# Transposing the second layer's q and k with VectorE and GpSimd in place of TensorE, in a two-layer encoder trunk

## The chip, the core and the metric

The kernel runs on one core of one Trainium2 chip. The engines are named as in the profile: PE is TensorE (PEld its weight load), DVE VectorE, ACT ScalarE, POOL GpSimd, SP the engine whose queue issues the loads. The metric is the device time in microseconds of one execution, and lower is better. Kernels are compared by the median of several runs.

## The reference, cut to what matters

Two layers, 256 tokens, 2048 channels, all in float32. Each layer normalises and modulates its input, multiplies it by one wide matrix, and gets from that two attention mixers and two gates; after the gated merge comes an output projection and a gated feed-forward part with a short convolution. The change is in the second layer's q and k, between their norm and the scores:

```python
h = rmsnorm(x, norm_mix[l]) * (1.0 + sc_a) + sh_a
qa, ka, va, qb, kb, vb, ga, gb = split_cols(h @ w_in[l])
qa = rotary_partial(rmsnorm(qa.reshape(B, S, HA, HEAD_DIM), qn_a[l]), pos)
ka = rotary_partial(rmsnorm(ka.reshape(B, S, GA, HEAD_DIM), kn_a[l]), pos)
ya = window_attention(qa, ka, va, sink_a[l]) @ w_proj_a[l]
qb = rmsnorm(qb.reshape(B, S, HB, HEAD_DIM), qn_b[l])
kb = rmsnorm(kb.reshape(B, S, HB, HEAD_DIM), kn_b[l])
yb = neighbourhood_attention(qb, kb, vb, rel_bias_b[l]) @ w_proj_b[l]
merged = jax.nn.sigmoid(ga) * ya + jax.nn.sigmoid(gb) * yb
```

Mixer A has 8 query heads and 2 key heads of 128 channels, mixer B 8 and 8.

## The kernel before

**The stream of weights.** All matrices are read once, as 128x128 blocks in the order in which they are used. Sixteen blocks are a unit. `unit_steps` loads a unit (SP's queue), and splits each of its halves into two tiles: a cast by ACT (L319, `hl<-w`) and the difference between the weights and that cast by DVE (L320). A product is then three matmuls, high by high, high by low and low by high. The half units are called by layer, unit and half: `hl1_35_0` is the first half of unit 35 of the second layer. There are four such buffers, so the cast of a half can begin when PE has left the half two units earlier.

**q, k and v.** In the second layer units 0 to 7 belong to gate columns; units 8 to 43 make nine groups of 512 columns, four units each (`Stream.tokens`, L399 to L401, 24 matmuls a unit, into PSUM tiles `ps1_8` to `ps1_40`): group 0 holds both k heads of A and v, groups 1 and 2 the q heads of A; 3 and 6 are k of B, 5 and 8 q of B, 4 and 7 v of B. Then the gate units follow.

**Work in the background.** After each unit `Stream.tick` runs what was deferred by one tick and moves background jobs on by their rates (`Paced`). For a group of q or k, `qk_rows` sums squares per head on ACT (L569), takes roots (`qss` on DVE, L462, and `qrs` on POOL, L463), and three ticks later multiplies by the roots on DVE (`norm`, L578, into `qn`), with the rotary part for mixer A. One tick later `turn` transposes head by head on PE into PSUM (`qtp`, L602), and ACT writes the result with the gain to its place (L603). `qn` has one buffer.

**The heads.** `attention` starts a head when its groups are ready and moves all live heads on by one step at a time, `ATT` steps a tick. A head splits q and k into high and low parts (`in_halves`, `split`: ACT L411, DVE L412), makes scores on PE (`sc`, L629), a softmax on DVE and ACT (L632 to L648), transposes the probabilities, and multiplies by v (`po`, L667). In the second layer the probabilities are already transposed off PE, for all heads: `turned_blocks` transposes 32x32 blocks on DVE (L293) and moves the blocks with 16 copies on POOL (L298, `p<-packA`, `p<-packB`, `p<-spare`), and one step later `split` makes `pT` of them. The transposed rows of a head lie where q of the two heads before was, so DVE's transposition waits until POOL has copied the head before.

**The order.** Each engine runs its instructions in the order of the built program. The framework puts them in an order of its own from the priorities and dependences; `tc.keep_in_program_order` holds single instructions where the program has them.

Of the kernel before, what the change touches and what calls it, by code (L numbers as in the profile page):

```python
# [9 lines left out]
F32 = mybir.dt.float32  # L10
# [5 lines left out]
P = 128  # L16
# [4 lines left out]
HEAD = 128  # L21
# [57 lines left out]

H_RATE = [2.7, 1.7]  # L80

ATT = [1.288, 0.43]
ATT_B = [0.21, 0.4]

SCORES_3 = (1,)

MOVED = [(0,0), (8,8)]
STEPS = [1, 1]

# [49 lines left out]
def encoder(ctx: ExitStack, tc: tile.TileContext, a: dict, out: bass.AP):  # L139
# [144 lines left out]
    def later(n, fn):  # L284
# [3 lines left out]
        else:  # L288
            bg.defer(lambda: later(n - 1, fn))

    def turned_blocks(src, rows, n):

        nc.vector.transpose(out=rows, in_=src)  # L293
        blocks = rows.rearrange("p t (n k) -> p n t k", n=n)
        dst = src.rearrange("p t (n k) -> p (t n k)", n=n).rearrange("p (n t k) -> p n t k", n=n, t=2)
        for b in range(0, P, BLOCK):
            for a in range(0, P, BLOCK):
                nc.gpsimd.tensor_copy(  # L298
                    out=dst[a : a + BLOCK, :, :, b : b + BLOCK], in_=blocks[b : b + BLOCK, :, :, a : a + BLOCK]
                )  # L300

    def unit_steps(l, u, by_halves=False):

# [101 lines left out]
                    self.tick()  # L405
            return pss

    def split(dst, src, scale=None):

        if scale is None:  # L410
            nc.scalar.copy(dst[:, 0], src)  # L411
            nc.vector.tensor_tensor(out=dst[:, 1], in0=src, in1=dst[:, 0].bitcast(F32), op=ALU.subtract)  # L412
            return
        nc.scalar.activation(out=dst[:, 0], in_=src, func=AF.Copy, scale=scale)
        nc.vector.scalar_tensor_tensor(
            out=dst[:, 1], in0=src, scalar=scale, in1=dst[:, 0].bitcast(F32), op0=ALU.mult, op1=ALU.subtract
        )
# [140 lines left out]
            nc.vector.tensor_tensor(out=z[:], in0=ps[:, :S], in1=self.rbs[:], op=ALU.mult)  # L558
            return z, sh

    def qk_rows(pss, heads, rot, gain, dst, then):

        cols = 0
        n = heads * HEAD
        ss = sm.tile([P, 8], F32, name="qss", tag="qss")
        for t, ps in enumerate(pss):
            for i in range(heads):
                sq = at.tile([P, HEAD], F32, name="qsq", tag="qsq", bufs=1)
                nc.scalar.activation(  # L569
                    out=sq[:], in_=ps[:, cols + i * HEAD : cols + (i + 1) * HEAD], func=AF.Square,  # L570
                    accum_out=ss[:, t * heads + i : t * heads + i + 1],
                )
        rs = sm.tile([P, 8], F32, name="qrs", tag="qrs")
        rsqrt(rs[:, : 2 * heads], ss[:, : 2 * heads], HEAD, 2 * heads)
        def norm():
            qn = at.tile([P, 2, 4, HEAD], F32, name="qn", tag="qn", bufs=1)
            for t, ps in enumerate(pss):
                nc.vector.tensor_tensor(  # L578
                    out=qn[:, t, :heads],
                    in0=ps[:, cols : cols + n].rearrange("p (h d) -> p h d", d=HEAD),  # L580
                    in1=rs[:, t * heads : (t + 1) * heads].unsqueeze(2).broadcast_to([P, heads, HEAD]),
                    op=ALU.mult,
                )
            if rot is not None:
                x1, x2 = qn[:, :, :heads, :HALF], qn[:, :, :heads, HALF:ROT]
# [12 lines left out]
        def turn(qn):  # L598
            for t in range(2):
                ps = ax.tile([P, 4, P], F32, name="qtp", tag="ax")  # L600
                for h in range(heads):
                    nc.tensor.transpose(ps[:, h], qn[:, t, h], ident[:])  # L602
                nc.scalar.activation(  # L603
                    out=dst[:, :, t * P : (t + 1) * P], in_=ps[:, :heads], func=AF.Identity, scale=gain
                )
            then()

        bg.defer(lambda: bg.defer(lambda: bg.defer(norm)))
# [15 lines left out]
    def attend(q, k, v, p, mask, scale, sink, o, rows=None):  # L624

        sc = ax.tile([P, 2, S], F32, name="sc", tag="ax")
        for t in range(2):
            for i, j in by(q):
                nc.tensor.matmul(sc[:, t], q[i][:, t * P : (t + 1) * P], k[j], start=i + j == 0, stop=(i, j) == by(q)[-1])  # L629
        m = sm.tile([P, 2], F32, name="m", tag="m")  # L630
        for t in range(2):
            nc.vector.tensor_tensor_reduce(  # L632
                out=p[:, t], in0=sc[:, t], in1=mask[:, t], scale=scale, scalar=-3.0e38 if sink is None else sink,
                op0=ALU.add, op1=ALU.max, accum_out=m[:, t : t + 1],
            )
        nm = sm.tile([P, 2], F32, name="nm", tag="nm")
        nc.vector.tensor_scalar(out=nm[:], in0=m[:], scalar1=-1.0, scalar2=None, op0=ALU.mult)
        den = sm.tile([P, 2], F32, name="den", tag="den")
        for t in range(2):
            nc.scalar.activation(out=p[:, t], in_=p[:, t], func=AF.Exp, bias=nm[:, t : t + 1], accum_out=den[:, t : t + 1])  # L640
        if sink is not None:
            es = sm.tile([P, 2], F32, name="es", tag="es")
            nc.scalar.activation(out=es[:], in_=nm[:], func=AF.Exp, bias=sink)
            nc.vector.tensor_tensor(out=den[:], in0=den[:], in1=es[:], op=ALU.add)
        ri = sm.tile([P, 2], F32, name="ri", tag="ri")
        nc.vector.reciprocal(out=ri[:], in_=den[:])
        for t in range(2):
            nc.scalar.activation(out=p[:, t], in_=p[:, t], func=AF.Copy, scale=ri[:, t : t + 1])  # L648
# [12 lines left out]
        split(pT, tp[:])  # L661
        v = v()
        yield
        po = ax.tile([P, 512], F32, name="po", tag="ax")
        for i, j in by(v):
            for b in range(2):
                nc.tensor.matmul(po[:, :S], v[i][:, b], pT[:, j, b], start=i + j + b == 0, stop=i + b == 2)  # L667
# [118 lines left out]
    for l in range(L):  # L786
# [87 lines left out]

        def attention():

            todo = [(3, head_a, i) for i in range(HA)] + [(6 + 3 * (i // 4), head_b, i) for i in range(HB)]
            live = []
            while todo or live:
                for head in list(live):  # L880
                    if next(head, bg) is bg:
                        live.remove(head)
                        heads[0] += 1
                if todo and ready[0] >= todo[0][0]:
                    live.append(todo[0][1](todo[0][2]))
                    next(live[-1])
                    todo.pop(0)
                yield
# [15 lines left out]
        for pi, (groups, gates) in enumerate(parts):  # L904
            last = pi == len(parts) - 1
            for g, part in enumerate(groups):
# [21 lines left out]
                    for t in range(2):  # L928
                        nc.scalar.copy(rows[:, t, vcol:], pss[t][:, vcol:])
                if g == 0:  # L930
                    qk_rows(pss, GA, rots[1], gains[:, 1:2], kTa, turned)
                elif g < 3:
                    qk_rows(pss, 4, rots[0], gains[:, 0:1], dst, turned)
                elif vcol is None:
                    qk_rows(pss, 4, None, gains[:, 3:4] if g in (3, 6) else gains[:, 2:3], dst, turned)
                else:
                    turned()
                if g == 2:
                    bg.add(job, ATT[l])


# [240 lines left out]
```

## Time and profile before

| | us |
|---|---|
| median of 3 runs | 2658.42 (2656.88 to 2659.82) |
| the profiled execution's own time | 2660.64 |
| its span in the profile | 2658.7 |

The page gives the busy time of each engine, groups of instructions by line, and the chain of work that ended last. A timeline row has the start in us from the span's beginning, the duration, engine, line, operation, output and inputs, a count, and in brackets the idle time before it with what ended it. A waits row names who waited for whom, the total, the number of times and the longest. A windows row has the window and its length, then busy time and count for PE, PEld, DVE, ACT and POOL, the granted clock, DMA's share and GB/s.

### The profile page before, as it was taken

To read this page: it belongs to the slowest core of one execution; us is meant where nothing else is said; L and a number is where in the kernel's file an instruction comes from. 1 tells how busy PE (TensorE), PEld (TensorE's weight loads), DVE (VectorE), ACT (ScalarE), POOL (GpSimd) and SP (SyncE) were. 2 spreads that over 40 slices of the span, in tenths; PEclk is the share of its full clock that TensorE was granted. 3 is DMA by queue.
4 is the path that set the end of the run, shared out by engine and by line. 5 is a ranking of instruction groups with operands and counts; after the bars stand their busy time and mean duration, and the time that the engine had idled before them with its cause. 6 is when DMAs were issued, how large, how long until landed. Compare 5 with 4: busy or idle time off the path is not lost.

```text
span 2658.7 us, 51010 instructions
## 1 busy us (share of the span) xinstructions
PE 2646.4 (100%) x21192; PEld 2561.3 (96%) x21192; DVE 2116.5 (80%) x2975; ACT 1407.9 (53%) x2284; POOL 194.0 (7%) x281
## 2 busy tenths in 40 slices
PE   9999999999999999999999999999999999999999
PEld 7888899999999999999998889999999999999999
DVE  8898998897987888788886677868888866655664
ACT  5445865456653555355554566645565445544553
POOL 0001100000000000000000177610000000000000
PEclk9999999999999999999999999999999999999999
DMA  9988779885778788877856666766747775555554
GB/s 359 350 329 300 257 296 353 319 327 193 283 294 297 282 293 296 297 288 285 296 213 255 237 236 235 255 256 260 279 180 286 295 254 191 191 197 193 196 190 143
DMA packets 102042, 700.43 MB, mean 263 GB/s; under 512 B 12721, under 2 KB 15025, under 8 KB 17969
## 3 DMA queue, kind: packets, MB, share of 16 engines
q1 hardware_dynamic: 101810, 697.17, 71.3%
q8 instruction: 166, 2.72, 0.4%
q14 instruction: 66, 0.54, 0.1%
HBM read 695.03 MB, written 2.10 MB: 262 GB/s over the span
## 4 chain that ended last, share of the span: by engine, by line
PE 88%; DVE 5%; POOL 2%; ACT 2%; DMA 1%; issue 1%; DVEq 0%; ACTq 0%; POOLq 0%
PE ps L336 26%; PE ps L338 26%; PE ps L337 26%; PE ps_t L401 3%; PE ps_t L400 3%; PE ps_t L399 3%; POOL p L298 2%; DVE hl L320 2%; DMA aw<-in_aw 1%; DVE aw L230 1%; ACT hl L319 1%; PE sc L629 1%; PE po L667 1%; POOL qrs L463 0%; ACT qsq L569 0%
## 5 line engine op out<-in xcount | busy, mean ns | idle before, releaser
L320 DVE TENSOR_TENSOR hl<-w,hl 128x1024 fp32r<-128x1024 f32 x928 | 1129.8, 1224 | 308.6 <-ACT hl L319 304.6
L319 ACT CAST hl<-w 128x1024 fp32r<-128x1024 f32 x928 | 969.7, 1048 | 704.7 <-PE ps L338 494.0
L336 PE MATMUL ps<-h,hl 128*128 128x256 f32 x3328 | 922.5, 277 | 1.3 <-DVE ya L948 0.6
L337 PE MATMUL ps<-h,hl 128*128 128x256 f32 x3328 | 919.7, 276 | 0.0
L338 PE MATMUL ps<-h,hl 128*128 128x256 f32 x3328 | 919.6, 277 | 0.0
L336 PEld LDWEIGHTS ps<-h,hl 128*128 128x128 f32 x3328 | 624.8, 188 | 2.3 <-DVE ya L948 0.8
L337 PEld LDWEIGHTS ps<-h,hl 128*128 128x128 f32 x3328 | 625.2, 188 | 0.4 <-DVE h L492 0.2
L338 PEld LDWEIGHTS ps<-h,hl 128*128 128x128 f32 x3328 | 624.3, 188 | 0.0
L230 DVE CUSTOM_DVE_ANT_0 aw<-aw,cact,ab 128x2048 f32<-128x2048 f32 x189 | 443.8, 2349 | 73.8 <-DMA aw<-in_aw 73.4
L399 PE MATMUL ps_t<-hl,h 128*128 128x512 f32 x576 | 223.4, 393 | 2.1 <-ACT h L491 1.6
L400 PE MATMUL ps_t<-hl,h 128*128 128x512 f32 x576 | 224.9, 391 | 0.4
L401 PE MATMUL ps_t<-hl,h 128*128 128x512 f32 x576 | 224.3, 390 | 0.0
L1027 DVE SCALAR_TENSOR_TENSOR u<-ps,cw,u 128x255 f32<-128x255 f32 x304 | 146.1, 481 | 63.0 <-ACT u L1025 58.9
L1025 ACT ACTIVATE u<-ps,cw 128x256 f32<-128x256 f32 x152 | 85.7, 564 | 157.0 <-PE ps L338 156.9
L336 PE MATMUL ps<-merged,hl 128*128 128x256 f32 x512 | 141.8, 278 | 0.8 <-DVE m L425 0.8
L338 PE MATMUL ps<-merged,hl 128*128 128x256 f32 x512 | 141.7, 277 | 0.0
L337 PE MATMUL ps<-merged,hl 128*128 128x256 f32 x512 | 141.7, 277 | 0.0
L337 PE MATMUL ps<-act_o,hl 128*128 128x256 f32 x512 | 141.4, 276 | 0.0
L338 PE MATMUL ps<-act_o,hl 128*128 128x256 f32 x512 | 141.4, 276 | 0.0
L336 PE MATMUL ps<-act_o,hl 128*128 128x256 f32 x512 | 141.2, 276 | 0.0
L399 PEld LDWEIGHTS ps_t<-hl,h 128*128 128x128 f32 x576 | 107.9, 188 | 25.4 <-ACT h L491 2.6
L400 PEld LDWEIGHTS ps_t<-hl,h 128*128 128x128 f32 x576 | 108.1, 188 | 24.0 <-DVE hl L320 2.1
(239 smaller groups left out, 4774.5 us busy)
## 6 DMA issues: line engine op xcount, KB each, us to landing
w<-in_ws SPq DMA_DIRECT2D x463, 1024.0 KB, 4.9
aw<-in_aw SPq DMA_DIRECT2D x189, 1024.0 KB, 6.1
p<-in_bias SPq DMA_DIRECT2D x16, 256.0 KB, 4.5
x<-in_xT SPq DMA_DIRECT2D x4, 512.0 KB, 5.4
aw_o<-in_aw SPq DMA_DIRECT2D x2, 1024.0 KB, 12.5
out<-x SPq DMA_DIRECT2D x16, 128.0 KB, 2.2
w<-in_ws SPq DMA_DIRECT2D x2, 512.0 KB, 11.8
aw_b<-in_aw SPq DMA_DIRECT2D x1, 1024.0 KB, 17.1
```

Of the source, the lines that this page charges most:

```text
L230: nc.vector.tensor_tensor_reduce(out=raw[:], in0=raw[:], in1=cact[:], scale=1.0, scalar=ab[:, i : i + 1], op0=ALU.mult, op1=ALU.add, accum ...
L298: nc.gpsimd.tensor_copy(out=dst[a : a + BLOCK, :, :, b : b + BLOCK], in_=blocks[b : b + BLOCK, :, :, a : a + BLOCK])
L319: nc.scalar.copy(hl[:, 0], r)
L320: nc.vector.tensor_tensor(out=hl[:, 1], in0=r, in1=hl[:, 0].bitcast(F32), op=ALU.subtract)
L336: nc.tensor.matmul(out, hi, act[0], start=first, stop=False)
L337: nc.tensor.matmul(ps[:, :S], hi, act[1], start=False, stop=False)
L338: nc.tensor.matmul(out, lo, act[0], start=False, stop=last)
L399: nc.tensor.matmul(ps[:], xh, hi, start=kc == kcs[0], stop=False)
L400: nc.tensor.matmul(ps[:], xh, lo, start=False, stop=False)
L401: nc.tensor.matmul(ps[:], xl, hi, start=False, stop=kc == kcs[-1])
L1025: nc.scalar.activation(out=u, in_=ps, func=AF.Identity, scale=w[:, 1:2], bias=w[:, 3:4])
L1027: nc.vector.scalar_tensor_tensor(out=u[:, to], in0=ps[:, of], scalar=w[:, j : j + 1], in1=u[:, to], op0=ALU.mult, op1=ALU.add)
```

## The change

In the second layer `turn` no longer uses PE. DVE transposes the 32x32 blocks of `qn` in place (new line L612), POOL moves the blocks with 16 copies straight to their place in the pack (L298, as for the probabilities), and three ticks later (`QK_STEPS`) ACT multiplies there by the gain (`scaled`, L616). Only then do the heads count the group as ready. `qn` is laid out so that it can be transposed as one tile. Three kinds of instructions are held in program order: the products with the roots, the multiplication by the gain, and the cast that begins the split of a head's probabilities. Heads of mixer A may start one group earlier (`EARLY`, the job is added at group 1), at 0.40 steps a tick for 0.43. The first layer keeps its transposes on PE.

```diff
-ATT = [1.288, 0.43]
+ATT = [1.288, 0.4]
+EARLY = {1: 2}
+
+MOVED_QK = [(), (0,1,2,3,5,6,8)]
+QK_STEPS = 3
...
+    def moved_blocks(dst, src):
+
+        for b in range(0, P, BLOCK):
+            for a in range(0, P, BLOCK):
+                nc.gpsimd.tensor_copy(
+                    out=dst[a : a + BLOCK, :, :, b : b + BLOCK], in_=src[b : b + BLOCK, :, :, a : a + BLOCK]
+                )
...
-            nc.scalar.copy(dst[:, 0], src)
+            high = nc.scalar.copy(dst[:, 0], src)
+            if held:
+                tc.keep_in_program_order(high)
...
-            qn = at.tile([P, 2, 4, HEAD], F32, name="qn", tag="qn", bufs=1)
+            qn = at.tile([P, 8 * HEAD], F32, name="qn", tag="qn", bufs=1)[:, : 2 * n]
+            qn = qn.rearrange("p (t h d) -> p t h d", t=2, d=HEAD)
             for t, ps in enumerate(pss):
-                nc.vector.tensor_tensor(
-                    out=qn[:, t, :heads],
+                product = nc.vector.tensor_tensor(
+                    out=qn[:, t],
...
+                if moved:
+                    tc.keep_in_program_order(product)
...
         def turn(qn):
+            if moved:
+                nc.vector.transpose(out=qn, in_=qn)
+                moved_blocks(dst.rearrange("p h (t s) -> p h t s", t=2), qn.rearrange("p t h d -> p h t d"))
+
+                def scaled():
+                    tc.keep_in_program_order(nc.scalar.activation(out=dst, in_=dst, func=AF.Identity, scale=gain))
+                    then()
+
+                later(QK_STEPS, scaled)
+                return
...
-        split(pT, tp[:])
+        split(pT, tp[:], held=rows is not None)
...
-            todo = [(3, head_a, i) for i in range(HA)] + [(6 + 3 * (i // 4), head_b, i) for i in range(HB)]
+            todo = [(EARLY[l] + i // 4, head_a, i) if l in EARLY else (3, head_a, i) for i in range(HA)] + [(6 + 3 * (i // 4), head_b, i) for i in range(HB)]
...
-                if g == 2:
+                if g == (1 if l in EARLY else 2):
                     bg.add(job, ATT[l])
```

How the engines' orders change is read from the built programs. POOL first, from the second layer's first roots to the last heads. Before (`qrs` are roots, `p` a head's probabilities, `x16` counts equal rows):

```order
L463 TENSOR_TENSOR qrs<-qss,mhalf 128x4
L463 TENSOR_TENSOR qrs<-qss,mhalf 128x8 x3
L298 COPY p<-spare_16763 32x4x32 x16
L298 COPY p<-packA_15812 32x4x32 x17
L463 TENSOR_TENSOR qrs<-qss,mhalf 128x8
L298 COPY p<-packA_15812 32x4x32 x31
L463 TENSOR_TENSOR qrs<-qss,mhalf 128x8
L298 COPY p<-packA_15812 32x4x32 x48
L463 TENSOR_TENSOR qrs<-qss,mhalf 128x8
L298 COPY p<-packA_15812 32x4x32 x16
```

And after, from group 3's copies (those from `qn`) on:

```order
L298 COPY packB_0_15813<-qn 32x8x32 x16
L298 COPY p<-spare_16754 32x4x32 x16
L298 COPY p<-packA_15812 32x4x32 x32
L472 TENSOR_TENSOR qrs<-qss,mhalf 128x8
L298 COPY packB_0_15813<-qn 32x8x32 x16
L298 COPY p<-packA_15812 32x4x32 x16
L472 TENSOR_TENSOR qrs<-qss,mhalf 128x8
L298 COPY p<-packA_15812 32x4x32 x16
L298 COPY packB_1_15814<-qn 32x8x32 x16
L298 COPY p<-packA_15812 32x4x32 x32
L472 TENSOR_TENSOR qrs<-qss,mhalf 128x8
L298 COPY p<-packA_15812 32x4x32 x16
```

Four sets of 16 copies of twice the size now stand among the heads' sets, and the roots of group 5 stand behind all of head 2's copies, no longer behind the first of them (the 17th of the row with `x17`).

DVE between the differences of units 34 and 35, where group 5 (`ps1_28`) is multiplied by its roots. Before:

```order
L320 TENSOR_TENSOR hl1_34_0_17071<-w1_34_17069,hl1_34_0_17071 128x1024
L293 STREAM_TRANSPOSE packA1_15812<-p_16895 128x512
L462 TENSOR_SCALAR qss_16924<-qss_16924 128x8
L578 TENSOR_TENSOR qn_17101<-ps1_28_t0_16693,qrs_16941 128x512
L320 TENSOR_TENSOR hl1_34_1_17074<-w1_34_17069,hl1_34_1_17074 128x1024
L578 TENSOR_TENSOR qn_17101<-ps1_28_t1_16694,qrs_16941 128x512
L320 TENSOR_TENSOR hl1_35_0_17110<-w1_35_17108,hl1_35_0_17110 128x1024
```

After:

```order
L327 TENSOR_TENSOR hl1_34_0_17099<-w1_34_17097,hl1_34_0_17099 128x1024
L471 TENSOR_SCALAR qss_16952<-qss_16952 128x8
L327 TENSOR_TENSOR hl1_34_1_17102<-w1_34_17097,hl1_34_1_17102 128x1024
L588 TENSOR_TENSOR qn_17129<-ps1_28_t0_16720,qrs_16969 128x512
L588 TENSOR_TENSOR qn_17129<-ps1_28_t1_16721,qrs_16969 128x512
L612 STREAM_TRANSPOSE qn_17129<-qn_17129 128x1024
L327 TENSOR_TENSOR hl1_35_0_17138<-w1_35_17136,hl1_35_0_17138 128x1024
```

Both products and the new transposition stand together, ahead of the first difference of unit 35; the head's transposition has moved up, ahead of these rows.

ACT around the first cast of unit 43, where group 6 is multiplied by its gain. Before:

```order
L319 COPY hl1_42_1_17567<-w1_42_17562 128x1024
L669 COPY oA1_2_16804<-po_17467 128x256
L411 COPY pT_17476<-p_17235 128x512
L411 COPY vA1_1_17479<-packA1_15812 128x256
L411 COPY qA1_7_17523<-packA1_15812 128x256
L319 COPY hl1_43_0_17596<-w1_43_17594 128x1024
```

After:

```order
L418 COPY pT_17515<-p_17214 128x512
L418 COPY vA1_1_17518<-packA1_15812 128x256
L418 COPY qA1_7_17562<-packA1_15812 128x256
L616 ACTIVATE packB1_1_15814<-packB1_1_15814,gains1_15948 128x1024
L326 COPY hl1_43_0_17636<-w1_43_17634 128x1024
```

The multiplication by the gain now stands directly ahead of a cast that PE will need; it can begin when POOL's copies of group 6 have landed.

More of the change, by code (lines that the diff above doesn't have):

```diff
@@ L295, in turned_blocks @@
         dst = src.rearrange("p t (n k) -> p (t n k)", n=n).rearrange("p (n t k) -> p n t k", n=n, t=2)
[L296 to L300, printed above, removed]
+        moved_blocks(dst, blocks)
     def unit_steps(l, u, by_halves=False):
@@ L406, in tokens, with split @@
             return pss
-    def split(dst, src, scale=None):
+    def split(dst, src, scale=None, held=False):
         if scale is None:
-            nc.scalar.copy(dst[:, 0], src)
+            high = nc.scalar.copy(dst[:, 0], src)
+            if held:
+                tc.keep_in_program_order(high)
             nc.vector.tensor_tensor(out=dst[:, 1], in0=src, in1=dst[:, 0].bitcast(F32), op=ALU.subtract)
@@ L559, in level, with qk_rows @@
             return z, sh
-    def qk_rows(pss, heads, rot, gain, dst, then):
+    def qk_rows(pss, heads, rot, gain, dst, then, moved=False):
         cols = 0
@@ L583, in norm @@
                 )
+                if moved:
+                    tc.keep_in_program_order(product)
             if rot is not None:
-                x1, x2 = qn[:, :, :heads, :HALF], qn[:, :, :heads, HALF:ROT]
+                x1, x2 = qn[:, :, :, :HALF], qn[:, :, :, HALF:ROT]
                 tab = [rot[:, i].unsqueeze(2).broadcast_to([P, 2, heads, HALF]) for i in range(4)]
@@ L930, in encoder @@
                 if g == 0:
-                    qk_rows(pss, GA, rots[1], gains[:, 1:2], kTa, turned)
+                    qk_rows(pss, GA, rots[1], gains[:, 1:2], kTa, turned, g in MOVED_QK[l])
                 elif g < 3:
-                    qk_rows(pss, 4, rots[0], gains[:, 0:1], dst, turned)
+                    qk_rows(pss, 4, rots[0], gains[:, 0:1], dst, turned, g in MOVED_QK[l])
                 elif vcol is None:
-                    qk_rows(pss, 4, None, gains[:, 3:4] if g in (3, 6) else gains[:, 2:3], dst, turned)
+                    qk_rows(pss, 4, None, gains[:, 3:4] if g in (3, 6) else gains[:, 2:3], dst, turned, g in MOVED_QK[l])
                 else:
                     turned()
-                if g == 2:
+                if g == (1 if l in EARLY else 2):
                     bg.add(job, ATT[l])
```

## The prediction, as it was made

> **What bounds the kernel now.** I read the page's head first, then the waits of TensorE (PE) in the stretch that the change touches, the second layer's q/k/v stage with its attention, 1412 to 1760 us.
>
> ```profile
> span 2658.7 us, 51010 instructions
> PE 2646.4 (100%) x21192; PEld 2561.3 (96%) x21192; DVE 2116.5 (80%) x2975; ACT 1407.9 (53%) x2284; POOL 194.0 (7%) x281
> PE sc L629 <- ACT packB L603: 0.4, 1, 0.4
> ```
>
> The last line is all that PE waits there: 0.4 us in 348. So PE's own list of work sets the end, and whatever leaves that list is gained in full, as long as nothing comes late for PE. What can come late is seen in the busy time by stretch (the first five columns: window, length, PE, PEld, DVE, then ACT and POOL) and in two waits:
>
> ```profile
> 1465.00:1488.00 23.00, 23.00 (x107) 19.09 (x106) 14.91 (x21) 12.57 (x29) 1.64 (x1) 1.00 0.72 270
> 1534.00:1557.00 23.00, 23.00 (x110) 19.30 (x109) 19.36 (x37) 15.09 (x39) 20.91 (x30) 1.00 0.68 232
> 1582.00:1606.00 24.00, 24.00 (x117) 20.17 (x116) 18.54 (x32) 15.76 (x30) 20.96 (x37) 1.00 0.62 226
> ACT pT L411 <- POOL p L298: 5.8, 1, 5.8
> DVE packA L293 <- POOL p L298: 3.1, 4, 1.5
> ```
>
> GpSimd (POOL) is idle while the first q/k groups run (1.64 of 23 us), but when the heads of mixer A have begun it is busy 20.91 of 23 and 20.96 of 24 us, and ScalarE (ACT) and VectorE (DVE) already wait for it. The change puts four of its seven groups' copies into that stretch. That is the question of this case.
>
> **What the change removes.** The chain of waits gives PE's share:
>
> ```profile
> 1441.87 0.44 PE qtp L602 x4
> 1442.31 0.23 PE ps_t L399
> 1464.15 0.87 PE qtp L602 x8
> 1510.28 0.87 PE qtp L602 x8
> 1522.10 0.71 PE sc L629 x6
> 1651.40 0.68 PE po L667 x6
> L603 ACT ACTIVATE packB<-qtp,gains x16: 669/689/695, 289.7 to 1633.9; 128x512 f32<-128x512 f32 x16
> L319 ACT CAST hl<-w 128x1024 fp32r<-128x1024 f32 x928 | 969.7, 1048 | 704.7 <-PE ps L338 494.0
> ```
>
> Seven groups are turned: one of two heads (4 transposes, 0.44 us) and six of four (8 each, 0.87 us): 0.44 + 6 x 0.87 = 5.7 us leave PE. The wait of 0.4 us above was for such a turned group and goes too. That is 6.1 us, 0.23% of the span, and nothing else in the edit shortens PE's list. The rows also give PE's clock of units: four units from 1442.31 to 1464.15, 5.46 us each; a head's scores (sc) add 0.71, its output product (po) 0.68. On ACT 14 evacuations of some 0.69 us become 7 multiplications by the factor of 1024 elements, the size of a cast (1.05 us): less work, off the path.
>
> **What it adds.** On POOL 112 copies, for each group of four heads 16 of twice the old size; on DVE seven transpositions in place. What 16 copies cost is read from POOL's timeline and from single copies against DVE's:
>
> ```profile
> 1511.04 8.18 POOL L298 COPY p<-spare 32x128 f32<-32x128 f32 x16 [15.99 <-DVE spare L293]
> 1530.43 11.20 POOL L298 COPY p<-packA 32x128 f32<-32x128 f32 x16 [11.22 <-issue]
> 1565.88 1.64 POOL L463 TENSOR_TENSOR qrs<-qss,mhalf 128x8 f32<-128x8 f32 x1
> 1590.14 9.55 POOL L298 COPY p<-packA 32x128 f32<-32x128 f32 x16 [0.81 <-DVE packA L293]
> 1534.48 1.30 DVE L320 TENSOR_TENSOR hl<-w,hl 128x1024 fp32r<-128x1024 f32 x1
> 1534.75 1.18 POOL p L298
> 1535.97 0.29 POOL p L298
> 1536.30 0.29 POOL p L298
> 1532.20 2.35 DVE L230 CUSTOM_DVE_ANT_0 aw<-aw,cact,ab 128x2048 f32<-128x2048 f32 x1 [0.77 <-DMA aw<-in_aw]
> L293 DVE STREAM_TRANSPOSE packA<-p 128x512 f32<-128x512 f32 x7 | 5.0, 711 | 4.1 <-POOL p L298 3.1 <-ACT p L648 1.0
> ```
>
> Rows of 512 elements are transposed in 711 ns, so 1024 take some 1.3, 8.5 us in all, in a stage where DVE idles 3.6 of 23 us at its fullest: nothing, unless the queue it stands in is late.
>
> A copy takes 0.29 us, 0.33 from start to start. While DVE makes a difference of two tiles in SBUF (L320) the copy under way doesn't end: 1534.75 + 1.18 = 1535.93, 0.15 after the difference's 1535.78. So 16 copies take 16 x 0.33 = 5.3 us, plus about 0.95 for each L320 that falls among them and 2.1 for each L230: 5.3 + 4 x 0.95 = 9.1 for the row of 9.55, and 11.2 with one L230 for the row of 11.20. No row shows a copy of 256 elements. Its bounds are 0.33 (all of it fixed) and 0.61 (the 0.29 doubled). I take 0.45: of the 0.15 after the release, which surely moves the data, 0.12 is taken to double. [...]
>
> **The queue that decides.** POOL takes its work in order: group 3's copies, then head 0's, 1's, 2's, then group 5's roots (qrs), 5's copies, head 3, group 6's roots, head 4, 6's copies, head 5. DVE's products with the roots stand in front of the next unit's difference and wait for qrs, as now:
>
> ```profile
> 1541.66 0.71 DVE L293 STREAM_TRANSPOSE packA<-p 128x512 f32<-128x512 f32 x1 [0.52 <-POOL p L298]
> 1544.36 0.69 DVE L578 TENSOR_TENSOR qn<-ps_t,qrs 128x512 f32<-128x512 f32 x1 [1.93 <-POOL qrs L463]
> 1546.70 2.44 DVE L320 TENSOR_TENSOR hl<-w,hl 128x1024 fp32r<-128x1024 f32 x2
> 1554.26 1.21 DVE L320 TENSOR_TENSOR hl<-w,hl 128x1024 fp32r<-128x1024 f32 x1
> 1519.25 0.62 ACT L411 CAST pT<-p 128x512 fp32r<-128x512 f32 x1 [5.80 <-POOL p L298]
> 1519.77 3.89 ACT L319 CAST hl<-w 128x1024 fp32r<-128x1024 f32 x4
> 1528.33 0.90 ACT L648 ACTIVATE p<-p,ri 128x256 f32<-128x256 f32 x2
> ACT hl L319 <- PE ps_t L401: 16.3, 12, 2.0
> DVE p L632 <- DMA p<-in_bias: 0.9, 2, 0.7
> ```
>
> (1546.70 begins the difference of unit 35, 1554.26 that of 36. The row of ACT hl: a cast waits until PE has left the half unit two units back.) I walk the queue with these durations. PE's clock after the change: unit 28 starts at 1511.15 - 0.44 - 3 x 0.87 = 1508.1, unit 35, after two more scores and one output with scores, at 1508.1 + 7 x 5.46 + 2 x 0.71 + 1.39 = 1549.1; it needs its difference 0.23 later, at 1549.3.
>
> Unit 35: the cast 26_1 waits for PE's end of unit 24, 1508.1 - 0.71 - 3 x 5.46 = 1491.0; with its difference it is done at 1493.3. Behind it DVE has two products 1.3, an L230 2.35, a difference 1.2, head 0's maxima and small work 1.7, a difference 1.2 and group 3's transposition 1.3: 1502.3. POOL: group 3, 16 x 0.45 + 5 x 0.95 + 2.1 = 14.1, to 1516.4; head 0, 5.3 + 1.0, to 1522.7. ACT's cast pT 0.6 and head 1's scaling 0.9, DVE's transposition 0.7: 1524.9. Head 1, 5.3 + 6 x 0.95 + 2.1, and the next transposition 0.8: 1538.8. Head 2, 5.3 + 1.9: 1546.0. Roots 1.6, products 1.3, transposition 1.3, difference 1.2: 1551.5 with the hand-overs. PE waits 2.2 us. Now this difference is done at 1547.9, since qrs stands after one copy of head 2 and no group's copies are ahead.
>
> Unit 36: from the end of 35_1 to the start of 36_0 DVE needs 5.1 us now (1549.14 to 1554.26); so 36_0 ends at 1551.5 + 1.2 + 5.1 + 1.2 = 1559.0, and PE needs it at 1551.3 + 5.46 + 1.39 + 0.23 = 1558.4: 0.6 us.
>
> Unit 39: from 1550.3 POOL has group 5, 7.2 + 6 x 0.95 + 2.1 and about 1.2 for smaller pairs, to 1566.5; head 3, 5.3 + 1.9 + 2.1, to 1575.8; then roots, products, head 4's transposition and the difference 39_0, 4.9: 1580.7. PE needs it at 1558.8 + 3 x 5.46 + 1.39 + 0.23 = 1576.8: 3.9 us.
>
> Unit 43: POOL has head 4, 5.3 + 5 x 0.95 + 1.2, from 1579.5 to 1590.8 and group 6, 7.2 + 2.1 + 3 x 0.95 + 1.2, to 1604.2. The factor on ACT stands ahead of the cast 43_0: 1.05 + 1.05 + 1.2, 1607.5, while PE needs it at 1580.5 + 4 x 5.46 + 1.39 + 0.23 = 1604.0: 3.5 us. Head 5's copies, 5.3 + 0.95, hold head 6's transposition, which stands ahead of 43_1: 1604.2 + 6.2 + 0.8 + 1.2 = 1612.5 against 1610.3: 2.2 us.
>
> After that (gate units, no squares for groups) POOL catches up: ACT reaches group 8's factor near 1647, waits some 4 us, and the cast behind it is still 3 us early. The first three groups have 22 us of idle POOL each: nothing. On SP's queue the loads of mixer B's tables move behind one or two loads of weights; DVE waits 0.9 us for them now, and the scores that need them stand a unit later too: nothing. The rate of 0.40 ends the last head one unit later, long before its merge: nothing.
>
> Sum of stalls 2.2 + 0.6 + 3.9 + 3.5 + 2.2 = 12.4. Against the profiled execution's own time, 2660.64 (1.9 above its span): 2660.6 - 6.1 + 12.4 = 2666.9. That execution lies 2.2 above the median of 2658.42, so **2664.7, some 0.24% slower**. With copies at 0.33 three groups on the chain give back 3 x 1.9: 2659.0; at 0.61 they cost 3 x 2.6 more: 2672.5.
>
> **Rivals.**
> Hidden: POOL is in time everywhere and PE's 6.1 us are all kept: 2652.3. For it: heads start one unit earlier, the rate 0.40 spreads them a little more, while DVE waits POOL copies at 0.33 each, and only 0.4 us of waiting reach PE now. Against it: POOL's 20.91 of 23 us.
> Half: the waits of units 35 and 39 come (6.1 us), those on ACT's side don't, because POOL gains a few us where my count of L320 among its copies is too high: 2660.6 - 6.1 + 6.1 - 2.2 = 2658.4, no change.
> Dear copies: the larger copy costs 0.61 and also holds DVE. Now a difference that follows a copy grows from 1.22 to 1.30; some 18 differences stand in units 35 to 43, and 0.2 more for each is 3.6 us on the same chain: 2672.5 + 3.6 = 2676. [...]
>
> **Numbers.** A measurement of this kernel can tell about 0.2%, 5.3 us, from no change: faster is below 2653.1, slower above 2663.7. Forecast (2659 to 2673): 0.45, of it 0.36 slower, 0.09 same. Hidden: 0.23 (0.21 faster). Half: 0.18 (0.14 same, 0.03 faster, 0.01 slower). Dear: 0.14, slower. So slower 0.51, same 0.25, faster 0.24. The range that holds 8 in 10 runs from the hidden case to the dear one, 2652 to 2677; the forecast's own is 2659 to 2673.
>
> **What would show it.** Right: no qtp on PE and 52 fewer matmuls there; PE's waits in 1500 to 1620 us grow from nothing to some 12 us, most of it for hl L327 (DVE) at units 35, 39 and 43; DVE's products wait 3 us and more for qrs; ACT's factor waits for POOL's copies from qn; POOL is busy without a gap from 1502 to 1610. Copies of 256 elements of 0.40 us when DVE is idle confirm the price. Wrong: PE's waits stay under 2 us, or they lie with the B heads after 1640, where I expect none.

## The result, and the profile after

| | before | after |
|---|---|---|
| median | 2657.18 (22 runs) | 2660.86 (22 runs) |
| profiled execution's own time | 2660.64 | 2662.14 |
| its span | 2658.7 | 2660.4 |

The ratio is 1.0014, with a 95% interval of 1.0008 to 1.002: 3.7 us slower, real but within what the prediction called no change (up to 2663.7). The forecast was 2664.7.

The head of the changed kernel's page, then TensorE's waits from 1400 to 1780 us, then two rows of all engines' waits from 1490 to 1660 us:

```profile
span 2660.4 us, 51015 instructions
PE 2642.0 (99%) x21140; PEld 2555.1 (96%) x21140; DVE 2127.9 (80%) x2982; ACT 1411.1 (53%) x2277; POOL 279.9 (11%) x393
PE ps_t L407 <- DVE hl L327: 5.8, 4, 3.0
PE ps_t L406 <- ACT hl L326: 0.8, 1, 0.8
...
ACT packB L616 <- POOL packB L298: 10.4, 3, 7.3
DVE qn L588 <- POOL qrs L472: 10.1, 2, 5.5
```

The 52 transposes are gone (21192 matmuls before), and where PE waited 0.4 us it now waits 6.6 us. The rows under it are the chain that the prediction named: products (L588) for roots (L472), and ACT's factor (L616) for copies (L298). Lines after are 7 higher at the casts (L326), the differences (L327) and the token matmuls (L406 to L408).

At unit 35 DVE's timeline has the links in their order, products behind the root, the new transposition, then the difference:

```profile
1544.84 1.29 DVE L588 TENSOR_TENSOR qn<-ps_t,qrs 128x512 f32<-128x512 f32 x2 [5.52 <-POOL qrs L472]
1546.16 1.25 DVE L612 STREAM_TRANSPOSE qn<-qn 128x1024 f32<-128x1024 f32 x1
1547.33 2.52 DVE L327 TENSOR_TENSOR hl<-w,hl 128x1024 fp32r<-128x1024 f32 x2
```

Where PE stands, from its timeline (start, duration, matmul, and in brackets the idle time with its releaser):

```profile
1395.83 0.39 PE L406 MATMUL ps_t<-hl,h 128*128 128x512 f32 x1
...
1546.81 0.39 PE L406 MATMUL ps_t<-hl,h 128*128 128x512 f32 x1
1548.57 0.50 PE L407 MATMUL ps_t<-hl,h 128*128 128x512 f32 x1 [1.36 <-DVE hl L327]
...
1577.48 0.50 PE L407 MATMUL ps_t<-hl,h 128*128 128x512 f32 x1 [2.98 <-DVE hl L327]
...
1601.61 0.50 PE L406 MATMUL ps_t<-hl,h 128*128 128x512 f32 x1 [0.79 <-ACT hl L326]
1602.87 0.66 PE L407 MATMUL ps_t<-hl,h 128*128 128x512 f32 x1 [0.76 <-DVE hl L327]
1603.33 0.63 PE L408 MATMUL ps_t<-hl,h 128*128 128x512 f32 x1
...
1606.32 0.47 PE L406 MATMUL ps_t<-hl,h 128*128 128x512 f32 x1
1606.62 0.40 PE L407 MATMUL ps_t<-hl,h 128*128 128x512 f32 x1
```

Token matmuls follow each other every 0.227 us here (the median from 1396 to 1640 us). By that, the intervals around the waits are too long by 1.5 us at unit 35, 0.9 at unit 36 (1556), 3.1 at unit 39, 1.0 and 1.0 at the first half of unit 43, and 0.2 at its second: 7.7 us. The first row is where the groups' token matmuls begin; in the kernel before that is at

```profile
1398.06 0.39 PE L399 MATMUL ps_t<-hl,h 128*128 128x512 f32 x1
```

so this execution was 2.2 us ahead before the change had done anything. That must be taken off wherever times of the two are compared.

The last three rows of PE show something that no step foresaw: from 1602.87 to 1606.62 nine matmuls took 3.75 us instead of 2.04. The busy time by stretch has the reason in its column of the granted clock (third from the end):

```profile
1602.00:1604.00 2.00, 1.24 (x4) 0.94 (x4) 1.15 (x3) 1.46 (x6) 1.83 (x5) 0.76 0.04 8
1604.00:1606.00 2.00, 2.00 (x6) 1.54 (x6) 0.35 (x1) 2.00 (x4) 1.45 (x5) 0.50 0.00 0
```

PE's clock fell to 0.50, and the nine matmuls took 1.7 us more. So 7.7 + 1.7 = 9.4 us were lost, and 5.7 + 0.4 won: 3.3 us net, against 3.7 measured.

### The profile page after: what moved, and what is told of

Its sections match the earlier page's. It is cut to its first block, busy times and chain, and to the rows that moved or that the text cites. A ratio compares the mean times of both kernels' runs of the same rounds, so it can differ in the third digit from the quotient of the medians.

```text
span 2660.4 us, 51015 instructions
## 1 busy us (share of the span) xinstructions
PE 2642.0 (99%) x21140; PEld 2555.1 (96%) x21140; DVE 2127.9 (80%) x2982; ACT 1411.1 (53%) x2277; POOL 279.9 (11%) x393
## 4 chain that ended last, share of the span: by engine, by line
PE 83%; DVE 7%; POOL 4%; DMA 3%; issue 2%; ACT 1%; DVEq 0%; ACTq 0%; POOLq 0%; SPq 0%
PE ps L343 24%; PE ps L345 24%; PE ps L344 24%; PE ps_t L408 3%; PE ps_t L406 3%; PE ps_t L407 3%; DMA aw<-in_aw 3%; DVE hl L327 2%; POOL p L298 2%; DVE aw L233 2%; POOL packB L298 2%; ACT hl L326 1%; DMA w<-in_ws 1%; PE sc L651 0%; PE po L689 0%
## 5 line engine op out<-in xcount | busy, mean ns | idle before, releaser
L327 DVE TENSOR_TENSOR hl<-w,hl 128x1024 fp32r<-128x1024 f32 x928 | 1132.8, 1227 | 321.2 <-ACT hl L326 318.8
L326 ACT CAST hl<-w 128x1024 fp32r<-128x1024 f32 x928 | 969.9, 1049 | 712.7 <-PE ps L345 486.2
L406 PE MATMUL ps_t<-hl,h 128*128 128x512 f32 x576 | 223.9, 393 | 2.9 <-ACT h L500 1.6
L408 PE MATMUL ps_t<-hl,h 128*128 128x512 f32 x576 | 225.3, 392 | 0.0
L406 PEld LDWEIGHTS ps_t<-hl,h 128*128 128x128 f32 x576 | 108.4, 189 | 27.0 <-ACT h L500 2.7
## 6 DMA issues: line engine op xcount, KB each, us to landing
aw_o<-in_aw SPq DMA_DIRECT2D x2, 1024.0 KB, 12.4
```

The source lines that it names most:

```text
L326: nc.scalar.copy(hl[:, 0], r)
L327: nc.vector.tensor_tensor(out=hl[:, 1], in0=r, in1=hl[:, 0].bitcast(F32), op=ALU.subtract)
L406: nc.tensor.matmul(ps[:], xh, hi, start=kc == kcs[0], stop=False)
L408: nc.tensor.matmul(ps[:], xl, hi, start=False, stop=kc == kcs[-1])
```

## The experiments

Each variant is the changed kernel with the edit shown. "Before" in a ratio is the kernel before, run on the same chip.

### Which groups cost: only the first three, only the last four, none

```diff
-MOVED_QK = [(), (0,1,2,3,5,6,8)]
+MOVED_QK = [(), (0,1,2)]      e1_first3
+MOVED_QK = [(), (3,5,6,8)]    e2_late4
+MOVED_QK = [(), ()]           e4_paceonly
```

> Only groups 0, 1 and 2 of the second layer are turned by VectorE and GpSimd; groups 3, 5, 6 and 8 go back to TensorE's transposes and ScalarE's scaling; pace and program order stay as in the change. Theory (GpSimd's queue: copies of 256 elements stand ahead of copies and roots that heads and units wait for, and that costs 9.3 us of TensorE's waits between 1500 and 1640): the waits of matmuls for the differences there go (under 1.5 us against 5.8), the roots no longer stand behind head copies for 5 us, TensorE keeps its granted clock at 1602 to 1606, and the time is the one before less about 2.2 us of transposes: 2654 to 2656, ratio to before 0.9985 to 1.0. Rival (the new pace and the earlier start of the first heads cost it): the waits stay, and the time is 2660 to 2664, the change's own or above, since fewer transposes are saved.

> Only groups 3, 5, 6 and 8 are turned by VectorE and GpSimd; groups 0, 1 and 2 go back to TensorE's transposes; pace and program order stay as in the change. Theory (the copies of groups 3, 5 and 6 meet the first heads' copies in GpSimd's queue): TensorE's waits at 1546, 1577 and 1602 us of about 9 us in all remain, and only 4 x 0.87 = 3.5 us of transposes are saved, so the time is about 2660.9 + 2.2 = 2663, ratio to before 1.001 to 1.003. Rival (the first three groups carry a share of the cost): the time comes down, 2656 to 2659.

> No group is turned by VectorE and GpSimd: all 52 transposes are TensorE's, and of the change only the pace, the earlier start of the first heads and the program order of ScalarE's high halves stay. Theory (the cost is GpSimd's queue and not pace or order): the time is that of before within 0.1%, 2655 to 2660, and TensorE's waits between 1500 and 1640 sum to under 3 us. Rival (pace and order cost it): the waits of about 9 us are there without any moved copy, and the time is about 2657 + 7 = 2664 or more.

| | median us | ratio to before |
|---|---|---|
| first three | 2656.86 | 0.9994 [0.9985, 1.0003] |
| last four | 2669.00 | 1.0043 [1.0031, 1.0056] |
| none, new pace and order | 2662.37 | 1.0020 [1.0011, 1.0028] |

TensorE's waits, 1400 to 1780 us, in that order:

```profile
PE sc L651 <- ACT packB L625: 1.1, 1, 1.1
```

```profile
PE ps_t L407 <- DVE hl L327: 6.8, 6, 1.8
PE ps L345 <- DVE hl L327: 3.0, 1, 3.0
```

```profile
PE sc L651 <- ACT packB L625: 2.3, 1, 2.3
```

With the first three alone the waits for differences are gone (the time is 0.9 us above the expected 2654 to 2656, and one wait of 1.1 us for a score is left), with the last four alone they are all there: the cost lies with the last four, and by the places of the waits before 1611 us with groups 3, 5 and 6. The last four did worse than expected, since a new wait of 3.0 us stands there, up to 1638.8 us, beyond the place that the theory spoke of, and the granted clock is at 0.50 behind it, from 1638.9 us for 3.4 us. A maximum of mixer B's first head had waited 2.8 us on DVE for its table, up to 1627.7 us; DVE was busy from there to the late difference at 1637.5.

The third run was a miss. The theory called pace and order free, and they cost 4.3 us by themselves (2662.37 against 2658.08 on that chip). The wait is another one: a score (L651), 2.3 us, behind the multiplication that empties a TensorE transpose (L625). By the code both take their PSUM buffer from one pool, `ax`, and the profile names L625 as what released the score. That ACT instruction started at 1561.34, behind casts and a softmax. With 0.4 us for a difference, TensorE's waits are 2.7 us there against 0.4 before, so 2 of the 4.3 us are not accounted for. A moved group needs no such buffer. So the move of the first three groups is worth more under this pace than its 2.2 us of transposes: 2656.86 against 2662.37, 5.5 us. The pace and the earlier start were not tried apart.

### Group 6, and the program order of the products

Group 6 back on TensorE; the same with its products held in order; and all groups moved with no product held:

```diff
-MOVED_QK = [(), (0,1,2,3,5,6,8)]
+MOVED_QK = [(), (0,1,2,3,5,8)]          e3_no6, e5_no6_held
...
-                if moved:
+                if held:                e5_no6_held (true in the second layer)
                     tc.keep_in_program_order(product)
...
-                if moved:                e11_unheld
-                    tc.keep_in_program_order(product)
```

> As the change, but group 6 goes back to TensorE's transposes. Theory (the 16 copies of group 6 at 1587 to 1599 us put head 5's copies late, and these the two waits of about 1 us at 1602 and 1603 and with them the granted clock's drop to 0.50): the waits there go, the clock stays above 0.95 between 1600 and 1610, and the time is the change's less 2.0 us of waits less 2.4 us of slow matmuls plus 0.87 us of transposes: about 2657.3, ratio to before 0.999 to 1.001. Rival (the drop of the clock has nothing to do with these waits, and comes at that place anyway): the two waits go but the drop stays, the time is about 2659.7. Second rival (the copies of group 5 do it): both stay, 2661.7.

> As the experiment without group 6, but the products of all groups of the second layer, group 6 among them, stay in program order on VectorE, as they do in the change. Theory (without that order group 6's products moved ahead of differences in VectorE's queue and waited there for a root that stood behind head 3's copies on GpSimd; with it the waits up to 1580 us are those of the change, 1.5 + 0.9 + 3.1 us, and the two of 1 us at 1602 and the drop of the clock behind them are gone with group 6's copies): the longest wait for a difference is 3 us and not 4.9, and the time is 2660.9 - 4.4 + 0.9 = 2657.4, ratio to before 0.999 to 1.0005. Rival (order is not it; TensorE's transposes of group 6 bring a wait of their own for a PSUM buffer or for the products): a wait of 4 us or more stays near 1570, time 2661 to 2662.

> The change, but the products with roots are not kept in program order on VectorE; the copies, the pace and the program order on ScalarE stay. Theory (out of order the products move ahead of differences in VectorE's queue and wait there for roots that GpSimd's copies hold back): the longest wait of a matmul for a difference grows from 3.0 us to about 5 us, at group 6 as in the run where only that group was without this order, and the time is 2663 to 2667. Rival (the order of the products matters little, or costs): the longest wait stays at 3 us and the time is 2659 to 2662.

Measured: 2661.79 (1.0019 [1.0011, 1.0028]), 2661.30 (1.0009 [1.0, 1.0018]) and 2667.36 (1.0036 [1.0022, 1.005]). The first is a miss: less work for GpSimd, yet no gain. TensorE's waits of the run without group 6:

```profile
PE ps_t L407 <- DVE hl L327: 6.8, 3, 4.9
```

The 4.9 us are at unit 38, one earlier than in the change. DVE's timeline there shows what the experiment had changed unawares:

```profile
1572.98 0.69 DVE L588 TENSOR_TENSOR qn<-ps_t,qrs 128x512 f32<-128x512 f32 x1 [6.65 <-POOL qrs L472]
1573.59 1.22 DVE L327 TENSOR_TENSOR hl<-w,hl 128x1024 fp32r<-128x1024 f32 x1
```

Without the program order group 6's product had moved ahead of a difference, waited there 6.65 us for a root behind head 3's copies, and held the difference. The granted clock was at 0.50 for 3.4 us behind that wait, from 1574.3 us. With the order back, the profile of the second run is the one expected: three waits, 5.2 us in all, the longest 3.0, nothing at 1602, the clock at 1.0 throughout. Its executions spread from 2656.6 to 2664.5, and their median is 3.9 above the expected 2657.4. Only one was profiled, at 2659.36; why others took longer is open. The third run shows what the order is worth in the change as a whole: 1.0036 against 1.0014, some 5.8 us, with the same wait of 4.9 us, behind group 6's product, and the same fall of the clock, to 0.50 from 1571.7 us for 3.4 us (TensorE's waits, 1400 to 1780 us):

```profile
PE ps_t L407 <- DVE hl L327: 8.1, 4, 4.9
PE ps L345 <- DVE hl L327: 2.8, 2, 2.5
```

### Which copies hold the roots: heads of mixer A back on TensorE

```diff
+BACK = (0,1,2,3,4,5,6,7)    e8_heads_back
+BACK = (2,3)                e9_heads23_back
+BACK = (0,1,2,3,4,5)        e10_heads6_back
+BACK = (2,)                 e12_head2_back
...
-rows if i < MOVED[l][0] else None
+rows if i < MOVED[l][0] and not (l == 1 and i in BACK) else None
```

> The change, but the probabilities of the second layer's heads of kind A are turned by TensorE and evicted from PSUM, so that GpSimd has no head copies between the groups' copies and roots up to about 1640 us. Theory (GpSimd's queue holds the roots back, these the products, these the differences on VectorE): the waits for differences between 1500 and 1640 fall from 5.8 us to under 1.5 us, products wait for roots under 2 us each, and the time is 2660.9 - 9.3 of waits + 8 heads x 4 transposes x 0.11 = 3.5 us, so 2655 to 2657 (up to 2 us more if scores wait for a PSUM buffer). Rival (VectorE's and ScalarE's own load between 1540 and 1610 us makes the differences late, not GpSimd): waits of 5 us or more stay, and the time is 2663 to 2665.

> The change, but the probabilities of two heads of kind A only, heads 2 and 3, go back to TensorE's transposes: those whose copies stand ahead of the roots at 1543 and 1573 us in GpSimd's queue. Theory (a root behind a head's copies, then products behind the root, then differences behind the products): the waits at 1547, 1556 and 1574 us, 1.5 + 0.9 + 3.1 us, fall to under 1 us in all; those near 1602, behind group 6's copies, stay with the clock's drop; the time is 2660.9 - 5.0 + 2 x 4 x 0.11 = 2656.8, ratio to before 0.9985 to 1.0. Rival (the total load of GpSimd's queue makes the waits, whatever stands ahead of a root; 32 of some 240 copies less take away about a seventh): waits of 4 us or more stay before 1580, time 2660 to 2661.

> As the run with all eight heads of kind A back on TensorE, but heads 6 and 7 stay with VectorE and GpSimd. Theory (after group 6's copies no root waits for long, so the last two heads' copies cost nothing): no wait over 0.5 us between 1500 and 1640, two heads less than 8 on TensorE, time 2655.3 - 2 x 0.44 = 2654.4, ratio to before 0.998 to 0.9995. Rival (heads 6 and 7 behind group 6's copies make the waits near 1602): those waits and the clock's drop are there, time 2657 to 2659.

> The change, but of all heads only head 2's probabilities go back to TensorE's transposes; head 3's copies stay on GpSimd ahead of the second root. Theory (every root takes the place that the copies ahead of it leave: the first one 5.6 us earlier, as in the run without heads 2 and 3, then group 5's copies, head 3's and the second root, about 7 us earlier than in the change instead of 15): the waits of 1.5 and 0.9 us go, that of 3.1 us shrinks to under 1 us, and group 6's copies end early enough that those at 1602 and the clock's drop go too; the time is 2652.5 - 0.44 + at most 1.5 = 2652 to 2654. Rival (head 3's copies ahead of the second root are a cause of their own): the wait of 3.1 us and what follows at 1602 stay, time 2660.9 - 2.4 + 0.4 = 2658.9.

| heads on TensorE | median us | ratio to before |
|---|---|---|
| all eight | 2655.29 | 0.9988 [0.9979, 0.9996] |
| 2 and 3 | 2652.53 | 0.9980 [0.9972, 0.9989] |
| 0 to 5 | 2654.40 | 0.9988 [0.9979, 0.9996] |
| 2 | 2657.30 | 0.9998 [0.9989, 1.0007] |

With eight or six heads back, the view of TensorE's waits from 1400 to 1780 us has no row at all. GpSimd's queue was the cause, and not DVE's or ACT's own load. Two heads do as much, while DVE and ACT are busy for longer than in the change (the third and fourth busy times in the windows rows below). GpSimd's timeline of the change, and then of the run without heads 2 and 3 (the new line moves L298 to L299 and L472 to L473):

```profile
1535.89 7.20 POOL L298 COPY p<-packA 32x128 f32<-32x128 f32 x16 [0.81 <-DVE packA L304]
1543.17 1.63 POOL L472 TENSOR_TENSOR qrs<-qss,mhalf 128x8 f32<-128x8 f32 x1
1547.47 16.15 POOL L298 COPY packB<-qn 32x256 f32<-32x256 f32 x16 [2.67 <-DVE qn L612]
1563.68 8.98 POOL L298 COPY p<-packA 32x128 f32<-32x128 f32 x16
1572.74 1.64 POOL L472 TENSOR_TENSOR qrs<-qss,mhalf 128x8 f32<-128x8 f32 x1
1576.45 10.29 POOL L298 COPY p<-packA 32x128 f32<-32x128 f32 x16 [2.07 <-DVE packA L304]
1586.80 12.63 POOL L298 COPY packB<-qn 32x256 f32<-32x256 f32 x16
```

```profile
1539.50 1.63 POOL L473 TENSOR_TENSOR qrs<-qss,mhalf 128x8 f32<-128x8 f32 x1 [2.46 <-DVE qss L472]
1543.82 15.49 POOL L299 COPY packB<-qn 32x256 f32<-32x256 f32 x16 [2.68 <-DVE qn L613]
1559.68 1.63 POOL L473 TENSOR_TENSOR qrs<-qss,mhalf 128x8 f32<-128x8 f32 x1 [0.37 <-DVE qss L472]
1568.88 9.00 POOL L299 COPY p<-packA 32x128 f32<-32x128 f32 x16 [7.57 <-DVE packA L305]
1577.94 13.68 POOL L299 COPY packB<-qn 32x256 f32<-32x256 f32 x16
```

The roots come 3.7 and 13.1 us earlier on the profile's clock, though that execution was 1.9 us behind the change's at the first token matmul; they now wait for their own sums (`qss`) and for nothing else. Group 6's copies follow 8.9 us earlier, so unit 43 is in time too, which the expectation had denied: 2652.5 and not 2656.8. That is the whole saving kept: 2657.97 before on that chip, less 6.1, plus 0.9 for the transposes of two heads, makes 2652.8. TensorE's one wait left, and the busy time from 1500 to 1640 us of the change and of this run (PE's time and count come first):

```profile
PE po L690 <- ACT pT L419: 0.2, 1, 0.2
```

```profile
1500.00:1640.00 140.00, 133.31 (x729) 114.43 (x728) 103.38 (x160) 81.82 (x183) 121.61 (x186) 0.99 0.59 214
```

```profile
1500.00:1640.00 140.00, 139.81 (x807) 122.64 (x806) 110.23 (x172) 88.89 (x195) 113.34 (x163) 1.00 0.64 232
```

Head 2 alone is half of it, and missed the expected 2652 to 2654. The waits at units 35, 36 and 39 went as expected: group 5's copies start 4.4 us earlier than in the change, at 1543.04, and the second root comes at 1567.95. But head 3's copies, still ahead of it, hold up group 6's, which end at 1595.0 and not at 1591.6, and two waits near 1600 us remain:

```profile
PE ps_t L408 <- DVE hl L328: 2.4, 2, 1.6
```

### The pace of before

```diff
-ATT = [1.288, 0.4]
-EARLY = {1: 2}
+ATT = [1.288, 0.43]
+EARLY = {}
 MOVED_QK = (0,1,2,3,5,6,8) in e6_oldpace, (0,1,2) in e7_first3_old
```

> All seven groups moved as in the change, but the heads' pace and start are those of before (0.43, and the first heads once three groups are ready). Theory (the new pace alone cost 4.3 us in the run without moved copies because a score waited for a PSUM buffer that a scaling on ScalarE gave back late; the moved groups need no such buffer, so what the pace costs with them is only where heads' copies meet groups' copies in GpSimd's queue): waits for the differences of 4 to 12 us remain at other places, time 2657 to 2664, and TensorE's waits name VectorE's differences. Rival (the new pace costs 4.3 us whatever is moved): 2660.9 - 4.3 = 2656.6.

> Groups 0, 1 and 2 moved, pace and start of the heads those of before. Theory (the first three groups cost nothing and save 2.2 us of TensorE's transposes; the new pace's 1.3 us wait for a score at 1556 us goes): 2658.1 - 2.2 = 2655.9 or up to a microsecond less, ratio to before 0.998 to 1.0, waits between 1500 and 1640 as before, 1 us. Rival (the old pace puts head copies on GpSimd beside the groups' roots and costs as much as the new one): 2657 or more.

Measured: 2673.56 (1.0057 [1.0045, 1.007]) and 2663.40 (1.0017 [1.0008, 1.0026]); two misses. With all groups moved it lay beyond both theories: PE waits 7.9 us for differences of token units and 5.7 us in the units behind them (3.8 for differences, 1.9 for mixer A's output), and its clock is at 0.50 in two stretches of 6.8 us. The second run's rival was right, and its GpSimd shows why. Before, the root of group 5 stood after one copy of a head; here, without a single copy of a late group, the whole head stands ahead of it (first fence: before; second: this run, with PE's row that ends the wait):

```profile
1542.44 0.28 POOL L298 COPY p<-packA 32x128 f32<-32x128 f32 x1 [0.81 <-DVE qss L462]
1542.70 1.63 POOL L463 TENSOR_TENSOR qrs<-qss,mhalf 128x8 f32<-128x8 f32 x1
```

```profile
1541.40 6.18 POOL L298 COPY p<-packA 32x128 f32<-32x128 f32 x16 [5.22 <-DVE packA L304]
1547.66 1.64 POOL L472 TENSOR_TENSOR qrs<-qss,mhalf 128x8 f32<-128x8 f32 x1
1551.81 0.64 PE L407 MATMUL ps_t<-hl,h 128*128 128x512 f32 x1 [3.00 <-DVE hl L327]
```

## Why the prediction was right, and where it was off

**The mechanism and its places: right.** Root behind copies, products behind the root, difference behind the products; a factor behind copies with a cast behind it. The waits came at units 35, 36, 39 and 43, nowhere else, and none after 1640. Taking two heads' copies from in front of two roots removed nearly all of it. One sign did not come: GpSimd was not busy without a gap, it paused five times for 0.8 to 2.7 us between 1502 and 1610. And the case named as likeliest, slower than 2663.7 (0.51), did not come either, but no change (0.25): the links were right, their sum too large.

**The price of the copy: right.** The bounds were 0.33 and 0.61, the working value 0.45 from start to start, with 0.40 for a copy beside an idle DVE. The row of the copies from `qn` (least, median, most) has

```profile
L298 POOL COPY packB<-qn x64: 387/497/2522, 1499.4 to 1646.9; 32x256 f32<-32x256 f32 x64
```

Against 0.280, the least of the heads' copies of 128 elements here, 0.387 puts 0.107 us on the second 128, where 0.12 was taken. Sixteen copies of group 5 took 16.15 us for 16.2 worked out, of group 3 13.7 for 14.1.

**The walk of the queue: right in its steps, a little late.** Group 3's copies started at 1499.39 for 1502.3. Of the 2.9 us, 2.2 are this execution's lead; the other 0.7 stayed to unit 39, so that its stalls of 2.2 and 3.9 measured 1.5 and 3.1 (unit 36: 0.6 became 0.9).

**The terms of unit 43: the first too large.** 3.5 + 2.2 was forecast, and the waits are 1.0 + 1.0 and 0.2. Group 6's copies ended at 1599.43; the walk, less the lead of 2.2 us, has 1602.0. Of these 2.6 us, 0.9 were there when head 3's copies ended (1572.66 for 1573.6); the rest is head 4's and group 6's 16 copies, which took 10.29 and 12.63 us for 11.25 and 13.35. Factor, cast and difference then took what was charged, 1.05 + 1.05 + 1.2: the matmul that needed the difference started at 1602.87. PE itself came 0.9 us early, as it had stalled 5.5 us and not 6.7. So 3.5 became 2.0.

```profile
1599.47 1.15 ACT L616 ACTIVATE packB<-packB,gains 128x1024 f32<-128x1024 f32 x1 [7.30 <-POOL packB L298]
1600.53 1.03 ACT L326 CAST hl<-w 128x1024 fp32r<-128x1024 f32 x1
1605.65 0.71 DVE L304 STREAM_TRANSPOSE packA<-p 128x512 f32<-128x512 f32 x1 [2.47 <-POOL p L298]
1606.29 3.64 DVE L327 TENSOR_TENSOR hl<-w,hl 128x1024 fp32r<-128x1024 f32 x3
```

**The half clock: not foreseen, but it hid a wait that was.** The last two rows are the second term as forecast: head 5's copies hold head 6's transposition, and the first difference behind it (of the second half of unit 43) was done near 1607.5 (PE's next wait ends at 1607.52), late by GpSimd's copies and not by PE. At full clock PE would have asked for it 1.7 us sooner, near 1605.6, and waited some 1.9 us (an estimate from these rows); at half clock it waited 0.2. So the 1.7 us are no extra cost, but most of the 2.2 us forecast, in another form.

**The sum.** Stalls were forecast at 12.4 and came to 7.7 + 1.7 = 9.4, 3.0 less. The forecast also started from 2658.42, the median of 3 runs, where 22 runs give 2657.18. Together that is 4.2 us; the forecast, 2664.7, lay 3.8 above the measured 2660.86.

**Also unsaid:** the prediction costed the program order and the pace at nothing. Without the order the change would be 5.8 us slower. The pace and order alone cost 4.3 us, as long as the transposes still take PSUM buffers; with the moved groups the old pace is the dear one. The sum came out near the measurement without it because the walk followed the queues as they stood, whatever had put them so.

**The rivals.** "Hidden" fails with 6.6 us of waits. "Half" named 2658.4, which is nearer to the measured time than the forecast, but by waits of 6.1 us at units 35 and 39 alone; those were 4.6, and ACT's wait came too. "Dear copies" fails with 0.387, though its dearer differences show in part (up to 0.2 us on one, the last section).

## What to carry to other kernels

Moving work to an engine that is idle on average can still cost, if what stands behind it in that engine's order has no slack: here a root of 1.64 us sat behind 7 and 9 us of copies, and TensorE paid at the third hand-over. Look for the one small instruction on which others wait, and remove the work just ahead of it; two heads' copies given back won what eight did, and more, and gave 2652.53 us, faster than both kernels. An experiment that takes work out also changes the order of what stays: compare the order of the engines before reading its time.

## What the runs showed of the hardware

**The clock.** In the change it fell to 0.50 after two waits of 0.8 us, not after the single one of 3.0 us at 1574. In the run with the last four groups alone the same pair of waits left it at 1.00:

```profile
1604.99 0.49 PE L406 MATMUL ps_t<-hl,h 128*128 128x512 f32 x1 [0.81 <-ACT hl L326]
1606.26 0.50 PE L407 MATMUL ps_t<-hl,h 128*128 128x512 f32 x1 [0.77 <-DVE hl L327]
1606.00:1608.00 2.00, 1.74 (x8) 1.44 (x9) 0.53 (x3) 1.46 (x4) 1.79 (x6) 1.00 0.02 4
```

With the first three groups at the old pace it fell right behind one of 3.0 us:

```profile
1551.00:1553.00 2.00, 1.19 (x3) 1.00 (x4) 2.00 (x8) 0.00 (x0) 0.00 (x0) 0.75 0.00 0
```

So the length of one wait doesn't tell these cases apart. Read in steps of 0.1 us, the granted clock stays at 0.50 (0.43 us from matmul to matmul) for 3.4 us in five executions: from 1603.0 in the change, 1552.0 in the run just shown, 1574.3 without group 6, 1571.7 with no product held, and 1638.9 with the last four alone. With all groups at the old pace it does so twice for 6.8 us, from 1547.0 and from 1594.8, which lie 14 x 3.41 us apart. The clock's own record in the traces of the two kernels has the same step: in the change it has 1587.198 us at 1.00, then 3.412 at 0.50, then 1054.719 at 1.00 up to the next fall, 0.8 us behind the span; that is 465, 1 and 309 times 3.4133. In the kernel before it has 2641.916 us at 1.00, 774 times 3.4133. So wherever an execution's clock changed more than once here, the changes lie 3.41 us or a multiple of it apart.

What follows is an estimate from that spacing and the waits, with a grid of 3.41 us laid in each run from its own fall: what tells the cases apart may be how much of one step of the grid PE stood idle (the time between two matmuls less their usual 0.227 us). In the step before its fall that was 2.0 us in the change, and from 2.5 to 3.4 us in the six others. The wait at 1574 of the change falls into two steps with 1.4 and 1.7 us, the pair of the last-four run into two with 0.7 and 1.3, and the most that a step of the second layer's attention had without a fall, over all runs, is 1.8 us (from 1608.2 in the last-four run). All these runs fit a limit between 1.8 and 2.0 us of 3.41; no run was made to test it.

**Differences beside copies.** Among copies of 256 elements a difference took up to 1.38 and 1.41 us (those that start at 1499.48 and 1511.02), beside no copy 1.22, and behind a copy of 128 elements 1.30: it lost 0.2 us at most, while a copy of 256 elements took 0.387 us or more.
